# Up's block products with high and low operand halves in one matmul, and the norm factor applied in down

## The chip, the cores and the metric

The kernel runs on one core of a Trainium2 chip. The metric is the device time of one execution in microseconds; the median of several executions counts. The core has engines with queues of their own: TensorE (PE; its weight loads, PEld, overlap its matmuls), VectorE (DVE), ScalarE (ACT), GpSimd (POOL) and SyncE (SP, which issues most DMA transfers). They wait for each other through semaphores, and each takes its own queue in order.

## The reference, cut to what matters

One layer of a streaming encoder for 512 tokens and a model width of 2048. Token mixers and a cross-attention come first; the change concerns only the last step, the MLP:

```python
def _rmsnorm(x, gain, eps=NORM_EPS):
    y = xf * lax.rsqrt(jnp.mean(xf * xf, axis=-1, keepdims=True) + eps)
    return (y * gain.astype(jnp.float32)).astype(x.dtype)

hn = _rmsnorm(h, norm_mlp[l])
h = h + jnp.square(jax.nn.relu(hn @ mlp_w_up[l])) @ mlp_w_down[l]
out = _rmsnorm(h, norm_final)
```

`mlp_w_up` is 2048 x 8192 and `mlp_w_down` 8192 x 2048, all in 32-bit floats. The norm factor of a token, r = 1/sqrt(mean + eps), is a positive number, so relu(r u)^2 = r^2 relu(u)^2.

## The kernel before

**Precision.** A matmul here takes operands in a reduced 32-bit format (F32R). To keep the precision, each operand is split into a high half (a cast, on ScalarE) and a low half (operand minus high half, on VectorE): `split`, lines 128 to 136. A product then is three sums: high x high, high x low, low x high.

**Up.** `strassen` (line 1525) runs in 32 rounds, p = 0 to 31, of 256 output features each. It multiplies 2 x 2 blocks with seven block products in place of eight, named B11, B21, T1, T2, T3, B22, T4 by the operand on the activation's side (`comb`: seven combinations of eight tiles, made once; each tile holds the high half of 256 tokens in its columns HA and the low half in HB). The weights' side comes in each round: four 128 x 1024 blocks a11, a21, a22, a12 by DMA, and sums of them (s1, and in place) made by `add`, 1024 wide, on VectorE. `block` (line 1289) splits such an operand into tiles `whi` and `wlo`, two buffers each, and issues 24 matmuls of 256 columns: for each of 8 pieces of `whi`, one with HA and one with HB, then 8 pieces of `wlo` with HA. All 24 add up in the same 256 columns of a PSUM bank.

Three banks collect the products of a round: x takes B11, then T2, T3 and T4 on top, y takes T1 and then B22, z takes B21. After each product its sum so far is read: `S.copy` (ScalarE) or `add`/`sub` (VectorE) into the tiles c1 and c2 (128 x 512 each). A product that adds onto a bank waits until the reads of that bank are done. The products follow each other on TensorE as B11, T1, T2, B21, T3, B22, T4 (B21 is second in round 0). At the end of a round `done` (the function `square`, line 1652) makes c1 and c2 into relu(r c)^2: one VectorE operation (maximum or minimum with 0, times `rstd`, the factor r spread over all 128 rows, 512 tokens wide), and a Square on ScalarE. Four combinations of c1 and c2 follow on VectorE (tiles tt and t4), and DMA stores everything to a buffer in DRAM (`Cd`).

In round 0, `used` (line 1656) also computes r: a column sum by small matmuls (`pcol2`), Sqrt and reciprocal to the column tile `rcol`, and from it `rstd`: four diagonal tiles on VectorE, eight small matmuls into `prs` and a copy.

Beside this, rounds 2 to 17 transpose an old tile each on TensorE (`ht`, copied by ScalarE to `hr`), and up to round 30 a one-column copy to `ticks` lets GpSimd start background transfers.

**Down.** The stored tiles come back, are split, and `down` multiplies them with the down weights, again seven products, here with 512 output columns a matmul and tokens on the partitions. `into` (line 1698) adds finished banks to the residual tiles g, one VectorE addition of 128 x 512 each; the last product does the same in `last`. The final norm and the stores end the program.

**What sets the order.** A scheduler orders each engine's instructions when the program is built; the order below is the built program's.

Of the kernel before, what the change touches and what calls it, by code (L numbers as in the profile page):

```python
# [10 lines left out]
F32R = mybir.dt.float32r  # L11
# [6 lines left out]
P = 128  # L18
# [55 lines left out]
def build(tc, I, out):  # L74
# [1215 lines left out]
    def block(pt, a, parts, start):  # L1290
# [8 lines left out]
        for k in range(8):  # L1299
            PE.matmul(pt, lo[:, k * P:k * P + P], parts[k][0], start=False, stop=k == 7, skip_group_check=True)  # L1300

    def product(i, pt, a, start=True):
        block(pt[:, HA], a, [(comb[i][k][:, HA], comb[i][k][:, HB]) for k in range(8)], start)

# [220 lines left out]
    def strassen(p, done, used):  # L1525

        def product(i, pt, a, start=True):  # L1530
            block(pt[:, HA], a, [(comb[i][k][:, HA], comb[i][k][:, HB]) for k in range(8)], start)
            if used:
                used(i)

        if p == 0:
            a11, a12, a22, a21 = (raw(I["w_up"][p, i], o) for i, o in ((0, 1), (3, 1), (2, 1), (1, 0)))
        else:
            a11, a21, a22, a12 = (raw(I["w_up"][p, i]) for i in range(4))
        s1 = raw(None, 0 if p == 0 else None)
        x, y, z = (psb(f"up{n}{p}", t) for n, t in (("x", "mx"), ("y", "mg"), ("z", "mm")))  # L1540
        c1, c2 = sl2(), sl2()

# [12 lines left out]
        if p > 0:
            product(B21, z, a12)
            sub(c1[:, HA], c1[:, HA], z[:, HA])
        add(a12, a12, s1)
        product(T3, x, a21, False)
        add(c2[:, HB], c2[:, HB], x[:, HA])  # L1560
        product(B22, y, a12, False)
        add(c1[:, HB], c1[:, HB], y[:, HA])
        done(c1, ALU.min)
        product(T4, x, a22, False)
        S.copy(c2[:, HA], x[:, HA])  # L1565
        done(c2, ALU.max)
        t = pu.tile([P, T], F32, tag="tt", name=f"tt{p}", bufs=1)
        t4 = pu.tile([P, M], F32, tag="t4", name=f"t4_{p}", bufs=1)
        sub(t[:, HA], c1[:, HB], c1[:, HA])
        sub(c1[:, HB], c1[:, HB], c2[:, HB])  # L1570
        sub(t[:, HB], c1[:, HA], c1[:, HB])
        sub(t4, c2[:, HA], t[:, HB])
        if p > 1 and wanted:
            S.copy(ticks[:, p:p + 1], c2[:, 0:1])
            background(ticks[:, p:p + 1], 1)
        h = slice(p % 2 * M, p % 2 * M + M)
        v = lambda a: a.rearrange("p (a b) -> p a b", b=M)
        nc.scalar.dma_start(Cd[p // 2][:, 2:4, h], v(c2))
        nc.scalar.dma_start(Cd[p // 2][:, 0:2, h], v(c1))
        nc.sync.dma_start(Cd[p // 2][:, 4:6, h], v(t))  # L1580
        nc.sync.dma_start(Cd[p // 2][:, 6, h], t4)
# [65 lines left out]
        G[t][m] = ph.tile([P, 2, T], F32, tag=f"h{i // 2}{i % 2}", name=f"g{t}{m}", bufs=1)  # L1647
        nc.sync.dma_start(G[t][m], HTd[:, t, m * 1024:m * 1024 + 1024].rearrange("p (a b) -> p a b", b=T))

    diag = []  # L1650
    for p in range(32):
        def square(c, op):
            V.scalar_tensor_tensor(out=c, in0=c, scalar=0.0, in1=rstd, op0=op, op1=ALU.mult)
            S.activation(c, c, AF.Square)

        def used(i):
            if p == 0 and i == T3:
                pt = psb("pcol2", "scr", 1)
                for t in range(4):
                    op = PE.matmul(pt[:, t:t + 1], acc[:, t * P:(t + 1) * P], ones[:, 0:1], start=True, stop=True)  # L1660
                    if t == 0:
                        tc.keep_in_program_order(op)
                S.activation(rcol, pt[:, 0:4], AF.Sqrt, bias=b_eps6, scale=1.0 / 2048)
                V.reciprocal(out=rcol, in_=rcol)
                diag.append(sl2())
                for t in range(4):
                    V.tensor_scalar(out=diag[0][:, t * P:(t + 1) * P], in0=ident, scalar1=rcol[:, t:t + 1], scalar2=None, op0=ALU.mult)
            if p == 0 and i == B22:
                pt = psb("prs", "scg", 1)
                for t in range(4):  # L1670
                    op = PE.matmul(pt[:, t * P:(t + 1) * P], ones, diag[0][:, t * P:(t + 1) * P], start=True, stop=True)
                    if t == 0:
                        tc.keep_in_program_order(op)
                S.copy(rstd, pt)
            if p == 31 and i in (T1, T2, T3):
                for q in ((0,), (1, 2), (3,))[i - T1]:
                    piece_(0, 0, q)
# [20 lines left out]
    def into(half, blk, m, pts, op):  # L1698
        for t in (0, 1):
            g = G[2 * half + t][m][:, blk, :]  # L1700
            V.tensor_tensor(out=g, in0=g, in1=pts[t], op=op)

    def down(c, i, q, pts, a, start):
        cnt[0] += 1
# [41 lines left out]
    def last(c):  # L1746
        kept = {}
        done = [(t, n) for n in range(4) for t in (2, 3)]
        for t in (0, 1):
            for m, q in both:  # L1750
# [15 lines left out]
                        gained(1, n)  # L1766
                if q == 3:
                    g = G[t][m][:, 1, :]
                    V.tensor_tensor(out=g, in0=g, in1=X[m][t], op=ADD)
                    square_of(t, 1, m)  # L1770
                    if t == 1 and m == 0:
                        gained(1, 1)
# [185 lines left out]
```

## Time and profile before

| | |
|---|---|
| median of 3 runs | 2951.33 us (2949.74 to 2951.42) |
| profiled execution, its own time | 2950.02 us |
| its span | 2948.3 us |
| PE busy | 2914.1 us (99%) |
| PEld busy | 2538.3 us (86%) |
| DVE busy | 2163.4 us (73%) |
| ACT busy | 1530.7 us (52%) |
| POOL busy | 312.6 us (11%) |

The span is the profiled execution from first to last instruction; its own time is 1.7 us longer. Busy shares are means over stages: the projections and mixers take the first 1.3 ms, up runs from 1663 to 2324 us, down from there to the end. In the timelines, a row is start and length in us, engine, line, operation, out<-in, shape and count, and in brackets the idle time before it with what ended it.

### The profile page before, as it was taken

Reading aid. Unit: us, or ns where it says so; the run is one execution under the profiler, and the core shown is the slowest. Engines: PE = TensorE matmul, PEld = TensorE weight load, DVE = VectorE, ACT = ScalarE, POOL = GpSimd, SP = SyncE. Lnnn points to the kernel's source line nnn. Section 1 sums busy time; section 2 is a strip of 40 time slices with the busy share of each in tenths; the row PEclk is TensorE's granted clock in tenths of the full one; section 3 lists DMA queues with packets and bytes.
Section 4 is the critical chain, followed back from the end, with each engine's and each line's share of the span. In section 5 each row is a group of like instructions: output and inputs, shape, how many; then the busy total and the mean of one; then the engine's idle time right before and its main releaser. Section 6 shows DMA issues by size and latency. Waiting matters only on the chain.

```text
span 2948.3 us, 52595 instructions
## 1 busy us (share of the span) xinstructions
PE 2914.1 (99%) x20866; PEld 2538.3 (86%) x20866; DVE 2163.4 (73%) x3114; ACT 1530.7 (52%) x2160; POOL 312.6 (11%) x704
## 2 busy tenths in 40 slices
PE   9999999999999999999999999999999999999998
PEld 7887787787778898879988899999999878888887
DVE  7676676676677746767856788888888897878776
ACT  6554545555556555664445545454444555454544
POOL 0302203213113000001111000000100000000000
PEclk9999999999999999999999999999999999999999
DMA  5332433323425588787788667778777878686755
GB/s 180 107 92 79 105 87 84 98 88 85 125 79 154 160 257 303 243 268 203 197 224 194 177 192 214 216 221 249 210 196 204 270 263 268 215 264 220 253 187 189
DMA packets 304520, 546.93 MB, mean 186 GB/s; under 512 B 97224, under 2 KB 178380, under 8 KB 303248
## 3 DMA queue, kind: packets, MB, share of 16 engines
q1 hardware_dynamic: 245264, 449.17, 48.3%
q0 software_dynamic: 35840, 67.12, 11.2%
q10 hardware_dynamic: 23168, 27.27, 2.6%
q8 instruction: 164, 2.69, 0.4%
q14 instruction: 84, 0.69, 0.1%
HBM read 479.10 MB, written 131.48 MB: 207 GB/s over the span
## 4 chain that ended last, share of the span: by engine, by line
PE 61%; DMA 3%; DVE 3%; ACT 1%; issue 1%; SPq 0%; DVEq 0%; ACTq 0%
PE upx L1297 8%; PE upy L1297 4%; PE upx L1300 4%; PE dx L1711 3%; PE dx L1712 3%; PE dx L1714 3%; PE kq L249 3%; PE kp L249 3%; PE vp L122 3%; PE sc L122 3%; PE at L122 3%; PE vo L122 2%; PE opx L1297 2%; PE upy L1300 2%; PE upz L1297 2%; PE dy L1714 2%
## 5 line engine op out<-in xcount | busy, mean ns | idle before, releaser
L130 ACT CAST whi<-ub 128x1024 fp32r<-128x1024 f32 x291 | 305.5, 1051 | 358.3 <-PE upx L1297 87.3
L131 DVE TENSOR_TENSOR wlo<-ub,whi 128x1024 fp32r<-128x1024 f32 x291 | 355.1, 1222 | 76.4 <-ACT whi L130 72.3
L249 PE MATMUL py<-xhi,whi 128*128 128x512 f32 x928 | 370.8, 400 | 7.0 <-ACT xhi L249 7.0
L249 PE MATMUL py<-xhi,wlo 128*128 128x512 f32 x928 | 377.3, 407 | 0.0
L249 PE MATMUL py<-xlo,whi 128*128 128x512 f32 x928 | 371.8, 401 | 0.0
L130 ACT CAST whi<-ua 128x1024 fp32r<-128x1024 f32 x205 | 215.5, 1051 | 262.6 <-PE upx L1297 72.6
L249 ACT CAST whi<-wraw 128x1024 fp32r<-128x1024 f32 (+1 forms) x180 | 188.0, 1045 | 234.1 <-PE py L249 183.0
L249 DVE TENSOR_TENSOR wlo<-wraw,whi 128x1024 fp32r<-128x1024 f32 (+1 forms) x180 | 224.4, 1247 | 96.3 <-ACT whi L249 93.9
L131 DVE TENSOR_TENSOR wlo<-ua,whi 128x1024 fp32r<-128x1024 f32 x205 | 250.4, 1222 | 58.5 <-ACT whi L130 57.1
L1297 PE MATMUL upx<-cb,whi 128*128 128x256 f32 x2048 | 269.4, 285 | 1.5 <-ACT whi L130 1.5
L1297 PEld LDWEIGHTS upx<-cb,whi 128*128 128x128 f32 x2048 | 256.1, 193 | 1.8 <-ACT whi L130 1.7
L249 PEld LDWEIGHTS py<-xhi,whi 128*128 128x128 f32 x928 | 175.4, 189 | 41.0 <-ACT xhi L249 7.0
L249 PEld LDWEIGHTS py<-xlo,whi 128*128 128x128 f32 x928 | 175.1, 189 | 37.9 <-issue 1.0
L249 PEld LDWEIGHTS py<-xhi,wlo 128*128 128x128 f32 x928 | 175.5, 189 | 33.2 <-issue 1.0
L1711 PE MATMUL dx<-whi,dh 128*128 128x512 f32 x480 | 187.2, 390 | 1.3 <-ACT sl L1565 0.8
L1712 PE MATMUL dx<-whi,dl 128*128 128x512 f32 x480 | 186.8, 389 | 0.0
L1300 PE MATMUL upx<-cb,wlo 128*128 128x256 f32 x1024 | 143.8, 283 | 0.3 <-DVE wlo L131 0.3
L1297 PE MATMUL upy<-cb,whi 128*128 128x256 f32 x1024 | 133.7, 283 | 1.8 <-ACT whi L130 1.8
L131 DVE TENSOR_TENSOR wlo<-wraw,whi 128x1024 fp32r<-128x1024 f32 x80 | 97.9, 1224 | 48.6 <-ACT whi L130 47.2
L1300 PEld LDWEIGHTS upx<-cb,wlo 128*128 128x128 f32 x1024 | 132.1, 192 | 0.5 <-DVE wlo L131 0.5
L1297 PEld LDWEIGHTS upy<-cb,whi 128*128 128x128 f32 x1024 | 127.5, 192 | 2.2 <-ACT whi L130 2.2
L1714 PE MATMUL dx<-wlo,dh 128*128 128x512 f32 x480 | 128.6, 389 | 0.0
(865 smaller groups left out, 6681.6 us busy)
## 6 DMA issues: line engine op xcount, KB each, us to landing
ws<-in_w_dn POOLq DMA_DIRECT2D x128, 512.0 KB, 7.2
wraw<-in_w_in SPq DMA_DIRECT2D x116, 512.0 KB, 3.6
ua<-in_w_dn SPq DMA_DIRECT2D x108, 512.0 KB, 4.2
ub<-in_w_up SPq DMA_DIRECT2D x72, 512.0 KB, 4.8
ua<-in_w_up SPq DMA_DIRECT2D x56, 512.0 KB, 4.6
ub<-in_w_dn SPq DMA_DIRECT2D x52, 512.0 KB, 4.4
sl<-cd SPq DMA_DIRECT2D x104, 256.0 KB, 4.4
ub<-ws SPq DMA_DIRECT2D x52, 512.0 KB, 4.4
```

The lines of the kernel that those rows point to most:

```text
L122: PE.matmul(o, l, r, start=start, stop=stop)
L130: tie(S.copy(hi, src))
L131: V.tensor_tensor(out=lo, in0=src, in1=hi.bitcast(F32), op=ALU.subtract)
L249: f(*a, **k)
L1297: PE.matmul(pt, hi[:, k * P:k * P + P], x, start=start, stop=False, skip_group_check=True)
L1300: PE.matmul(pt, lo[:, k * P:k * P + P], parts[k][0], start=False, stop=k == 7, skip_group_check=True)
L1711: PE.matmul(pts[t], uh[:, x], hi[:, w], start=start and z == 0 and q == 0, stop=False, skip_group_check=True)
L1712: PE.matmul(pts[t], ul[:, x], hi[:, w], start=False, stop=False, skip_group_check=True)
L1714: PE.matmul(pts[t], uh[:, x], lo[:, w], start=False, stop=z == 1 and q == 3, skip_group_check=True)
```

## The change

Three things change in up and one in down.

1. `product` in `strassen` calls the new function `wide` instead of `block`. For each of 8 pieces of `whi` it issues one matmul with the whole `comb` tile, 512 columns, so that high x high lands in the bank's first half and high x low in its second; the 8 matmuls with `wlo` stay 256 columns wide. A product has 16 matmuls. The two halves of a bank must now be summed: each of the seven reads gets one more VectorE operation, 256 wide, that adds or subtracts the second half.
2. `square` no longer multiplies by `rstd`: it is Relu (with scale -1 for c1, 1 for c2) and Square, both on ScalarE. The 512-wide VectorE operation is gone.
3. In round 0, `rstd` is not made (no diagonal tiles, no `prs` matmuls, no copy); `rcol` is squared, and `nrcol` is its negative.
4. In down, `into` and `last` multiply the bank by a column of `rcol` or `nrcol` while they add it: a three-operand VectorE operation in place of the addition.

```diff
+    def wide(pt, a, parts, start):
...
+        split(a, hi, lo)
+        for k in range(8):
+            PE.matmul(pt, hi[:, k * P:k * P + P], parts[k], start=start and k == 0, stop=False, skip_group_check=True)
+        for k in range(8):
+            PE.matmul(pt[:, HA], lo[:, k * P:k * P + P], parts[k][:, HA], start=False, stop=k == 7, skip_group_check=True)
...
         def product(i, pt, a, start=True):
-            block(pt[:, HA], a, [(comb[i][k][:, HA], comb[i][k][:, HB]) for k in range(8)], start)
+            wide(pt, a, comb[i], start)
...
         product(B11, x, a11)
         S.copy(c1[:, HA], x[:, HA])
+        add(c1[:, HA], c1[:, HA], x[:, HB])
...
         product(T1, y, s1)
         S.copy(c2[:, HB], y[:, HA])
+        add(c2[:, HB], c2[:, HB], y[:, HB])
...
         product(T2, x, s1, False)
         S.copy(c1[:, HB], x[:, HA])
+        add(c1[:, HB], c1[:, HB], x[:, HB])
...
             product(B21, z, a12)
             sub(c1[:, HA], c1[:, HA], z[:, HA])
+            sub(c1[:, HA], c1[:, HA], z[:, HB])
...
         product(T3, x, a21, False)
         add(c2[:, HB], c2[:, HB], x[:, HA])
+        add(c2[:, HB], c2[:, HB], x[:, HB])
         product(B22, y, a12, False)
         add(c1[:, HB], c1[:, HB], y[:, HA])
-        done(c1, ALU.min)
+        add(c1[:, HB], c1[:, HB], y[:, HB])
+        done(c1, -1.0)
         product(T4, x, a22, False)
         S.copy(c2[:, HA], x[:, HA])
-        done(c2, ALU.max)
+        add(c2[:, HA], c2[:, HA], x[:, HB])
+        done(c2, 1.0)
...
-        def square(c, op):
-            V.scalar_tensor_tensor(out=c, in0=c, scalar=0.0, in1=rstd, op0=op, op1=ALU.mult)
+        def square(c, sign):
+            S.activation(c, c, AF.Relu, scale=sign)
             S.activation(c, c, AF.Square)
...
                 V.reciprocal(out=rcol, in_=rcol)
-                diag.append(sl2())
-                for t in range(4):
-                    V.tensor_scalar(out=diag[0][:, t * P:(t + 1) * P], in0=ident, scalar1=rcol[:, t:t + 1], scalar2=None, op0=ALU.mult)
-            if p == 0 and i == B22:
-                pt = psb("prs", "scg", 1)
...
-                S.copy(rstd, pt)
+                V.tensor_tensor(out=rcol, in0=rcol, in1=rcol, op=ALU.mult)
+                V.tensor_scalar(out=nrcol, in0=rcol, scalar1=-1.0, scalar2=None, op0=ALU.mult)
...
     def into(half, blk, m, pts, op):
         for t in (0, 1):
             g = G[2 * half + t][m][:, blk, :]
-            V.tensor_tensor(out=g, in0=g, in1=pts[t], op=op)
+            i = 2 * half + t
+            f = (nrcol if op is SUB else rcol)[:, i:i + 1]
+            V.scalar_tensor_tensor(out=g, in0=pts[t], scalar=f, in1=g, op0=ALU.mult, op1=ALU.add)
...
-                    V.tensor_tensor(out=g, in0=g, in1=X[m][t], op=ADD)
+                    V.scalar_tensor_tensor(out=g, in0=X[m][t], scalar=rcol[:, t:t + 1], in1=g, op0=ALU.mult, op1=ALU.add)
```

The scheduler's order at three places follows, before and after. On TensorE, product T4 of round 4: the last two pieces of its high half and the first four of its low half. Before:

```order
L1297 MATMUL upx4_18734<-cb4_6_17020,whi830_18919 128x256 x2
L1297 MATMUL upx4_18734<-cb4_7_17713,whi830_18919 128x256 x2
L1300 MATMUL upx4_18734<-cb4_0_17014,wlo830_18920 128x256
L1300 MATMUL upx4_18734<-cb4_1_17015,wlo830_18920 128x256
L1300 MATMUL upx4_18734<-cb4_2_17016,wlo830_18920 128x256
L1300 MATMUL upx4_18734<-cb4_3_17017,wlo830_18920 128x256
```

After:

```order
L1308 MATMUL upx4_18529<-cb4_6_17020,whi829_18672 128x512
L1308 MATMUL upx4_18529<-cb4_7_17713,whi829_18672 128x512
L1310 MATMUL upx4_18529<-cb4_0_17014,wlo829_18673 128x256
L1310 MATMUL upx4_18529<-cb4_1_17015,wlo829_18673 128x256
L1310 MATMUL upx4_18529<-cb4_2_17016,wlo829_18673 128x256
L1310 MATMUL upx4_18529<-cb4_3_17017,wlo829_18673 128x256
```

The pair of 256-column matmuls on one piece (x2) has become one of 512; the low half and the sequence of products are as they were.

On ScalarE, the end of round 4: the rows run from the cast for T1 of round 5 (`whi834`) to that for T2 (`whi835`); sl822 and sl823 are c1 and c2 of round 4, L1654 is Square, L1565 and L1544 read bank x. Before:

```order
L130 CAST whi834_19016<-ub70_18980 128x1024
L1654 ACTIVATE sl822_18737<-sl822_18737 128x512
L1565 COPY sl823_18738<-upx4_18734 128x256
L1642 COPY hr0_2_18969<-ht0_2_18964 128x512
L1654 ACTIVATE sl823_18738<-sl823_18738 128x512
L1574 COPY ticks_14226<-sl823_18738 128x1
L1578 DMA cd2_187<-sl823_18738 128x2x256
L1544 COPY sl831_18984<-upx5_18981 128x256
L130 CAST whi835_19046<-ub70_18980 128x1024
```

After, between the same two casts (now `whi833` and `whi834`), with c1 and c2 as sl821 and sl822; L1670 is Relu, L1671 Square:

```order
L130 CAST whi833_18755<-ub70_18726 128x1024
L1670 ACTIVATE sl821_18532<-sl821_18532 128x512
L1582 COPY sl822_18533<-upx4_18529 128x256
L1671 ACTIVATE sl821_18532<-sl821_18532 128x512
L1660 COPY hr0_2_18715<-ht0_2_18710 128x512
L1670 ACTIVATE sl822_18533<-sl822_18533 128x512
L1671 ACTIVATE sl822_18533<-sl822_18533 128x512
L1592 COPY ticks_14226<-sl822_18533 128x1
L1596 DMA cd2_187<-sl822_18533 128x2x256
L1597 DMA cd2_187<-sl821_18532 128x2x256
L1554 COPY sl830_18730<-upx5_18727 128x256
L130 CAST whi834_18778<-ub70_18726 128x1024
```

Two Relu operations have come in, and both stores of c1 and c2 now stand ahead of the cast for T2 (`whi834`), where one stood before. In rounds 3, 5, 10, 12 and 17 the Relu of c1 stands ahead of the cast for the next T1 as well.

On VectorE at the same place, from the read of B22 in bank y to the low half for T2 of round 5 (`wlo833`, 834 and 835 belong to B11, T1 and T2 of round 5). Before:

```order
L1263 TENSOR_TENSOR sl822_18737<-sl822_18737,upy4_18735 128x256
L131 TENSOR_TENSOR wlo833_18987<-ub66_18972,whi833_18986 128x1024
L1653 SCALAR_TENSOR_TENSOR sl822_18737<-sl822_18737,rstd_201 128x512
L131 TENSOR_TENSOR wlo834_19017<-ub70_18980,whi834_19016 128x1024
L1653 SCALAR_TENSOR_TENSOR sl823_18738<-sl823_18738,rstd_201 128x512
L1260 TENSOR_TENSOR tt4_18950<-sl822_18737 128x256
L1263 TENSOR_TENSOR ub70_18980<-ub70_18980,ub66_18972 128x1024
L1260 TENSOR_TENSOR sl822_18737<-sl822_18737,sl823_18738 128x256
L1260 TENSOR_TENSOR tt4_18950<-sl822_18737 128x256
L1260 TENSOR_TENSOR t4_4_18951<-sl823_18738,tt4_18950 128x256
L131 TENSOR_TENSOR wlo835_19047<-ub70_18980,whi835_19046 128x1024
```

After, with c1 and c2 as sl821 and sl822 and the three low halves as `wlo832`, 833 and 834:

```order
L1263 TENSOR_TENSOR sl821_18532<-sl821_18532,upy4_18530 128x256
L131 TENSOR_TENSOR wlo832_18733<-ub66_18718,whi832_18732 128x1024
L1263 TENSOR_TENSOR sl821_18532<-sl821_18532,upy4_18530 128x256
L131 TENSOR_TENSOR wlo833_18756<-ub70_18726,whi833_18755 128x1024
L1263 TENSOR_TENSOR sl822_18533<-sl822_18533,upx4_18529 128x256
L1260 TENSOR_TENSOR tt4_18696<-sl821_18532 128x256
L1263 TENSOR_TENSOR ub70_18726<-ub70_18726,ub66_18718 128x1024
L1260 TENSOR_TENSOR sl821_18532<-sl821_18532,sl822_18533 128x256
L1260 TENSOR_TENSOR tt4_18696<-sl821_18532 128x256
L1260 TENSOR_TENSOR t4_4_18697<-sl822_18533,tt4_18696 128x256
L1263 TENSOR_TENSOR sl830_18730<-sl830_18730,upx5_18727 128x256
L131 TENSOR_TENSOR wlo834_18779<-ub70_18726,whi834_18778 128x1024
```

The scalings by rstd are gone; the second read of y stands between the low halves of B11 and T1, the read of T4's second half (`sl822`<-`upx4`) behind the low half of T1, and the read of round 5's B11 (`sl830`<-`upx5`) ahead of the low half of T2.

More of the change, by code (lines that the diff above doesn't have):

```diff
@@ L1300, in block @@
             PE.matmul(pt, lo[:, k * P:k * P + P], parts[k][0], start=False, stop=k == 7, skip_group_check=True)
+    def wide(pt, a, parts, start):
+        cnt[0] += 1
+        hi = pw.tile([P, 1024], F32R, tag="whi", name=f"whi{cnt[0]}", bufs=NWS)
+        lo = pw.tile([P, 1024], F32R, tag="wlo", name=f"wlo{cnt[0]}", bufs=NWS)
+        split(a, hi, lo)
[3 more added lines that the diff above has]
+            PE.matmul(pt[:, HA], lo[:, k * P:k * P + P], parts[k][:, HA], start=False, stop=k == 7, skip_group_check=True)
     def product(i, pt, a, start=True):
@@ L1557, in strassen @@
             sub(c1[:, HA], c1[:, HA], z[:, HA])
+            sub(c1[:, HA], c1[:, HA], z[:, HB])
         add(a12, a12, s1)
@@ L1648, in held @@
         nc.sync.dma_start(G[t][m], HTd[:, t, m * 1024:m * 1024 + 1024].rearrange("p (a b) -> p a b", b=T))
-    diag = []
     for p in range(32):
-        def square(c, op):
-            V.scalar_tensor_tensor(out=c, in0=c, scalar=0.0, in1=rstd, op0=op, op1=ALU.mult)
+        def square(c, sign):
+            S.activation(c, c, AF.Relu, scale=sign)
             S.activation(c, c, AF.Square)
@@ L1664, in used @@
                 V.reciprocal(out=rcol, in_=rcol)
-                diag.append(sl2())
-                for t in range(4):
-                    V.tensor_scalar(out=diag[0][:, t * P:(t + 1) * P], in0=ident, scalar1=rcol[:, t:t + 1], scalar2=None, op0=ALU.mult)
-            if p == 0 and i == B22:
-                pt = psb("prs", "scg", 1)
[L1670 to L1673, printed above, removed]
-                S.copy(rstd, pt)
+                V.tensor_tensor(out=rcol, in0=rcol, in1=rcol, op=ALU.mult)
+                V.tensor_scalar(out=nrcol, in0=rcol, scalar1=-1.0, scalar2=None, op0=ALU.mult)
             if p == 31 and i in (T1, T2, T3):
```

## The prediction

> **What bounds the kernel now.** I read the stages first. The three rows are busy time by stage: the MLP's up stage from its second of 32 rounds on (two rows), then down. The columns are window, length, PE, PEld, DVE, ACT and POOL busy with their instructions, granted clock, DMA share, GB/s.
>
> ```profile
> 1690.00:2050.00 360.00, 359.71 (x3004) 359.51 (x3003) 296.55 (x353) 180.24 (x262) 30.18 (x47) 1.00 0.75 214
> 2050.00:2326.00 276.00, 275.28 (x2289) 274.66 (x2287) 230.45 (x276) 137.69 (x195) 24.23 (x37) 1.00 0.76 212
> 2326.00:2948.00 622.00, 610.86 (x2683) 502.75 (x2683) 485.34 (x541) 302.92 (x375) 0.00 (x0) 1.00 0.72 237
> ```
>
> In up TensorE is idle for 360.00 - 359.71 + 276.00 - 275.28 = 1.0 us of 636, at full clock. VectorE is busy 82 to 84% and ScalarE 50%. So a shorter stream on TensorE shortens this stage, as long as VectorE, which the change loads further, keeps up. That is the whole question, so I read TensorE's timeline through the end of round p = 4 (start, length, line, tiles, count). `ht` is the transpose of one old tile, which stands only in rounds 2 to 17.
>
> ```profile
> 1770.04 2.08 PE L1297 MATMUL upx<-cb,whi 128*128 128x256 f32 x16
> 1771.96 1.12 PE L1300 MATMUL upx<-cb,wlo 128*128 128x256 f32 x8
> 1772.92 0.60 PE L1638 MATMUL ht<-cst,h 128*128 128x128 f32 x4
> 1773.28 2.16 PE L1297 MATMUL upx<-cb,whi 128*128 128x256 f32 x16
> ...
> 1776.24 2.08 PE L1297 MATMUL upy<-cb,whi 128*128 128x256 f32 x16
> ...
> 1779.12 2.08 PE L1297 MATMUL upx<-cb,whi 128*128 128x256 f32 x16
> ```
>
> Starts count here, since the lengths overlap. One product (T1, 1776.24 to 1779.12) takes 2.88 us for 24 matmuls of 256 columns: **120.0 ns each**, 16 on the high half in 1.92 us and 8 on the low half in 0.96. `ht` adds 1776.24 - 2.88 - 1772.92 = 0.44 us. The same kernel has 512-column matmuls with a weight load each, just ahead of up; these are the first and last of a run of 36:
>
> ```profile
> 1654.70 0.39 PE L122 MATMUL at<-phi,whi 128*128 128x512 f32 x1
> ...
> 1662.63 0.39 PE L122 MATMUL at<-phi,wlo 128*128 128x512 f32 x1
> ```
>
> 35 steps in 7.93 us: **226.6 ns each**, 13.4 ns less than two of 256.
>
> **TensorE's part.** A product becomes 8 x 226.6 + 8 x 120.0 = 2773 ns, 1813 on the high half and 960 on the low: 107 ns less. 31 rounds of 7 products give 217 x 0.107 = **23.2 us**, if TensorE stays the bound.
>
> Round 0 is held by other things (below, its waits), so I count half its 0.75 us, 0.4. It also loses the eight small matmuls that spread the norm factor:
>
> ```profile
> 1670.40 2.18 PE L1297 MATMUL upy<-cb,whi 128*128 128x256 f32 x16 [1.64 <-ACT whi L130]
> 1673.61 1.21 PE L1300 MATMUL upy<-cb,wlo 128*128 128x256 f32 x8 [1.02 <-DVE wlo L131]
> ...
> 1687.66 1.05 PE L1671 MATMUL prs<-sl,cst 128*128 128x128 f32 x8
> 1688.46 2.15 PE L1297 MATMUL upx<-cb,whi 128*128 128x256 f32 x16
> ```
>
> 1688.46 - 1687.66 = **0.8 us** on TensorE's own stream. Round 0's first waits stem from weights that land late and from the last operand splits; the extra additions there may cost 1 us or free as much, and I put them at 0 with 2 us either side.
>
> **VectorE's part.** Durations come from the same place, the end of round 4:
>
> ```profile
> 1770.24 0.42 DVE L1263 TENSOR_TENSOR sl<-sl,upy 128x256 f32<-128x256 f32 x1 [0.21 <-PE upy L1300]
> ...
> 1773.24 1.22 DVE L131 TENSOR_TENSOR wlo<-ub,whi 128x1024 fp32r<-128x1024 f32 x1 [0.84 <-ACT whi L130]
> 1774.39 0.68 DVE L1653 SCALAR_TENSOR_TENSOR sl<-sl,rstd 128x512 f32<-128x512 f32 x1
> 1774.99 0.42 DVE L1260 TENSOR_TENSOR tt<-sl 128x256 f32<-128x256 f32 x1
> 1775.32 1.22 DVE L1263 TENSOR_TENSOR ub<-ub,ub 128x1024 f32<-128x1024 f32 x1
> 1776.46 0.42 DVE L1260 TENSOR_TENSOR sl<-sl,sl 128x256 f32<-128x256 f32 x1
> 1776.91 0.42 DVE L1260 TENSOR_TENSOR tt<-sl 128x256 f32<-128x256 f32 x1
> ```
>
> From start to start, a 1024-wide operation takes 1.15 us, a 512-wide one 0.60, a 256-wide one 0.33, and 0.46 where the next needs its result. A round has 11 wide ones (7 low halves, 4 sums), 3 reads of PSUM, 4 combinations and 2 scalings with rstd. The change adds 7 reads of PSUM and drops the scalings: 7 x 0.33 - 2 x 0.60 = **+1.1 us**. The new total is 11 x 1.15 + 14 x 0.33 + 2 x 0.13 = 17.5 us in a round of 7 x 2.773 = 19.4 (19.85 with `ht`): 90%. It fits with 1.9 us to spare, but waits in VectorE's fixed order must fit there too, so I walked the tightest place.
>
> **The tightest place** is the end of a round. Let H be the end of T4's high half (1771.96 above). ScalarE there:
>
> ```profile
> 1772.16 1.05 ACT L130 CAST whi<-ub 128x1024 fp32r<-128x1024 f32 x1 [1.83 <-PE upx L1297]
> 1773.12 0.63 ACT L1654 ACTIVATE sl<-sl 128x512 f32<-128x512 f32 x1
> 1773.65 0.35 ACT L1565 COPY sl<-upx 128x256 f32<-128x256 f32 x1
> 1773.90 0.59 ACT L1642 COPY hr<-ht 128x512 f32<-128x512 f32 x1
> 1775.10 0.63 ACT L1654 ACTIVATE sl<-sl 128x512 f32<-128x512 f32 x1 [0.62 <-DVE sl L1653]
> 1775.77 0.19 ACT L1574 COPY ticks<-sl 128x1 f32<-128x1 f32 x1
> 1775.77 0.37 ACTq L1578 DMA_DIRECT2D cd<-sl  x1
> ```
>
> Steps read off: TensorE's end to a reader, 0.20; cast to next 0.96, cast to its low half on VectorE 1.08; 512-wide function to next 0.53, to one that needs it 0.67; copy to next 0.25; DMA issue 0.37. In the changed order: cast for next T1 at H+0.20, Relu c1 1.16, copy c2 1.69, Square c1 1.94, `hr` 2.47. VectorE takes that T1's low half at H+1.28 and then the new addition to c2 at 2.43; that ends at 2.85, so Relu c2 starts at 3.00, Square c2 3.67, ticks 4.34, two DMA issues to 5.09, copy of the next c1 5.10, cast for the next T2 5.35, ready at 6.43. TensorE, undisturbed, comes to that T2 at H + 0.96 + 0.44 + 2 x 2.773 = 6.95. **It is in time by 0.5 us**, and the other new condition there, next c1's addition before T2 may write onto x, ends at about 5.9, 1.0 us early. Where T4 writes onto x after T3, the two additions to c2 with T4's low half between end 0.20 + 0.33 + 1.15 + 0.42 = 2.10 us after T3, and B22 gives 2.77: 0.7 us early. So the added waits cost nothing while VectorE is not behind; without that cover each 0.1 us of lateness costs 31 x 0.1 = 3.1 us.
>
> Five rounds (3, 5, 10, 12, 17) have Relu c1 ahead of the cast on ScalarE. It needs c1's last addition, at about H+0.45, so the cast is late by 0.8 and T2 by 0.2: 5 x 0.2 = **1.0 us lost**. Late weights are covered no worse: the one such wait in the steady rounds was a sum behind a load of 8.18 us,
>
> ```profile
> 1879.54 8.18 DMA ub<-in_w_up
> ```
>
> that cost TensorE 0.29 us,
>
> ```profile
> 1890.21 1.21 PE L1300 MATMUL upx<-cb,wlo 128*128 128x256 f32 x8 [0.29 <-DVE wlo L131]
> ```
>
> and this sum now stands later in VectorE's queue.
>
> **Where up meets down.** Down's first block writes onto the bank that T4 of the last round held:
>
> ```profile
> 2325.66 0.35 ACT L1565 COPY sl<-upx 128x256 f32<-128x256 f32 x1
> 2326.06 0.50 PE L1711 MATMUL dx<-whi,dh 128*128 128x512 f32 x1 [0.78 <-ACT sl L1565]
> ```
>
> TensorE waited 0.78 us for the copy; now it also waits for an addition on a VectorE that splits down's operands besides. Bounds: 0 (the addition ready by then) and two wide operations ahead of it, 2.3; I take **1.0 us**.
>
> **Down.** Its 108 additions turn into the three-operand form with a column factor:
>
> ```profile
> L1701 DVE TENSOR_TENSOR g<-g,dx 128x512 f32<-128x512 f32 x60 | 38.5, 683 | 17.9 <-PE dx L1714 17.9
> L1739 DVE SCALAR_TENSOR_TENSOR g<-g,rt,gain 128x512 f32<-128x512 f32 x12 | 8.2, 749 | 0.1
> ```
>
> 112 x (749 - 683) = 7.4 us on VectorE, which is idle for 137 us of this stage; only the last, with the final norm behind it, is on the path: 0.1 us.
>
> **The sum**, against the profiled execution (span 2948.3, its own time 2950.0): 23.2 + 0.4 + 0.8 - 1.0 - 1.0 - 0.1 = 22.3 us less, 2927.7. The median shown, 2951.3, is 1.3 above that execution, so I say **2929 us**. With round 0 at either end, the seam at 0 or 2.3 and the five rounds free or doubled, the forecast's own range is 2924 to 2934.
>
> **Rivals.**
> - *Part of it eaten by the ScalarE chain.* My walk has 0.5 us to spare; if issues or the extra functions take 0.8 us more than read off, each T2 waits 0.3: 31 x 0.3 = 9.3 us back, 2938. For it: eleven steps in a row, two kinds of them (Relu, a second issue) not in that order before. Against: each step has a row. 12%.
> - *VectorE becomes the bound.* If the operations don't overlap as the starts show, a round takes 11 x 1.22 + 14 x 0.42 = 19.3 us, and with the 0.84 us wait for the cast that stays, 20.1: as long as now, 2950. Against: 1774.99 to 1775.32 is 0.33 for an operation that lasts 0.42. 6%. [...]
> - *A 512-column matmul is no cheaper here than two of 256*, so the change doesn't do on TensorE what it says: 2950. The 36 rows above speak against it. 3%. The Trainium skill, "TensorE: Matmul & The Clock Gate", section "Back-to-back issue gap", has a warm gap of N/2.4 + 2.5 ns, so a pair would save 2.5 ns and the whole about 4.5 us, an estimate from that page; the trace has 13.4.
> - *Slower: a convoy at the end of each round.* The addition to c2 is new between T4 and Relu c2, and next T2's cast stands behind Relu, Square and the issues. If VectorE reaches it two wide operations late (2.3 us) in every round, T2 waits 2.3 - 0.5 = 1.8 and the round loses 1.05 net of its 0.75: 31 x 1.05 = 33 us, 2984. It decides against the change from 1.25 us late on. For it: 90% load in a fixed order. Against: 1.9 us of slack a round to catch up. 6%.
>
> **How the numbers follow.** Forecast 73%, the others as given. 0.2%, 5.9 us, is about what a measurement of this kernel can tell from no change. Faster by more: forecast and first rival, 85%; within: second and third, 9%; slower: the last, 6%. The range must hold 8 in 10: the forecast with 2 us more below, for a better round 0, and the first rival with some room: 2922 to 2943.
>
> **What would show it.** Right: the step between products 2.77 us; from round 1 on TensorE idle for little more than 1 us; VectorE at about 90% of up; down's seam wait near 1.8 us; the small matmuls gone. Wrong: TensorE waits at T2's first matmul for the cast (first rival) or at x for an addition (last), or VectorE without idle time in up (second), or a high half still at 1.92 us (third).

## The result, and the profile after

| | median | runs | fastest to slowest |
|---|---|---|---|
| before, same chips | 2950.53 us | 6 | 2947.09 to 2955.29 |
| after | 2935.57 us | 6 | 2934.69 to 2941.63 |

The ratio after/before is 0.9947, with a 95% interval of 0.9937 to 0.9958. The change saves 15 us. 2929 had been predicted, within 2922 to 2943: direction and range hold, but a third of the expected 22.3 us did not come. The time lies outside 2924 to 2934, the forecast's own range; the stated range holds it only through the room that it left for the first rival, which expected 2938. The profiled execution of after took 2936.28 us, its span is 2934.5.

The stages of the changed kernel, with the columns of the table that the prediction opens with; the first row is the same stretch as there, the second ends at 2310, shortly before up does (2314):

```profile
1690.00:2050.00 360.00, 357.21 (x2059) 313.45 (x2059) 318.24 (x452) 200.20 (x300) 27.51 (x48) 1.00 0.74 218
2050.00:2310.00 260.00, 258.68 (x1476) 226.73 (x1475) 234.04 (x333) 144.26 (x213) 20.72 (x37) 1.00 0.74 212
```

TensorE still bounds up, but is now idle for 4.1 us of 620, where it was 1.0 of 636; and 0.7 of that 1.0 was the wait where up meets down, so in up itself it was 0.3. VectorE is busy 88 and 90%, as forecast. So two questions stand: what a product takes, and where the idle time is. TensorE's timeline, changed kernel, T1, T2 and what follows:

```profile
1850.25 2.00 PE L1308 MATMUL upy<-cb,whi 128*128 128x512 f32 x8
1852.09 1.11 PE L1310 MATMUL upy<-cb,wlo 128*128 128x256 f32 x8
1853.05 2.00 PE L1308 MATMUL upx<-cb,whi 128*128 128x512 f32 x8
1854.89 1.12 PE L1310 MATMUL upx<-cb,wlo 128*128 128x256 f32 x8
1855.84 0.60 PE L1656 MATMUL ht<-cst,h 128*128 128x128 f32 x4
```

From start to start the high half takes 1.84 us, not 1.813, and the low half 0.95 to 0.96; over a round of seven products without `ht` (19.55 us) a product is **2.793 us, not 2.773**. The single starts in the trace, as means over the steps without a wait, show where: the eight wide matmuls (512 columns) take 233, 235, 229, 233, 231, 227, 227 and 227 ns, the eight narrow ones (256 columns) 114, 119 and then 120. The wide ones are slow behind the narrow ones of the product before.

The tightest place, ScalarE at the end of round 4 of the changed kernel. H, the end of T4's high half, is 1774.45 here:

```profile
1774.65 1.05 ACT L130 CAST whi<-ub 128x1024 fp32r<-128x1024 f32 x1 [1.74 <-DVE wlo L131]
1775.60 0.62 ACT L1670 ACTIVATE sl<-sl 128x512 f32<-128x512 f32 x1
1776.13 0.35 ACT L1582 COPY sl<-upx 128x256 f32<-128x256 f32 x1
1776.38 0.63 ACT L1671 ACTIVATE sl<-sl 128x512 f32<-128x512 f32 x1
1776.92 0.57 ACT L1660 COPY hr<-ht 128x512 f32<-128x512 f32 x1
1777.38 0.64 ACT L1670 ACTIVATE sl<-sl 128x512 f32<-128x512 f32 x1
1778.05 0.63 ACT L1671 ACTIVATE sl<-sl 128x512 f32<-128x512 f32 x1
1778.72 0.19 ACT L1592 COPY ticks<-sl 128x1 f32<-128x1 f32 x1
1778.72 0.40 ACTq L1596 DMA_DIRECT2D cd<-sl  x1
1779.21 0.44 ACTq L1597 DMA_DIRECT2D cd<-sl  x1
1779.69 0.37 ACT L1554 COPY sl<-upx 128x256 f32<-128x256 f32 x1 [0.79 <-DVE tt L1260]
1779.96 1.05 ACT L130 CAST whi<-ub 128x1024 fp32r<-128x1024 f32 x1
```

The walk forecast these starts after H: 0.20, 1.16, 1.69, 1.94, 2.47, 3.00, 3.67, 4.34, the issues to 5.09, 5.10, 5.35. Measured: 0.20, 1.15, 1.68, 1.93, 2.47, 2.93, 3.60, 4.27, the issues to 5.20, 5.24, 5.51. The cast for T2 is done at H + 6.56 and TensorE comes at H + 6.98: 0.42 us to spare, 0.5 forecast.

Down begins without a wait on the banks; up's last matmuls and down's first, changed kernel:

```profile
2313.33 1.11 PE L1310 MATMUL upx<-cb,wlo 128*128 128x256 f32 x8
2314.28 0.40 PE L1722 MATMUL dx<-whi,dh 128*128 128x512 f32 x1
2314.51 0.40 PE L1723 MATMUL dx<-whi,dl 128*128 128x512 f32 x1
```

Five stretches of the two profiled executions add up to the difference of the spans. B21 of round 1 (bank z) marks where the disturbed beginning of up ends; below, a round is counted from one B21 to the next:

| stretch | before | after | difference |
|---|---|---|---|
| ahead of up | 1662.9 | 1668.4 | +5.5 |
| up, to B21 of round 1 | 37.2 | 35.3 | -1.9 |
| up, from there to down (214 products) | 623.9 | 610.5 | -13.4 |
| down, first to last matmul | 616.0 | 611.4 | -4.6 |
| after the last matmul | 8.3 | 8.8 | +0.5 |
| span | 2948.3 | 2934.5 | -13.8 |

The first line is a surprise, since the order of instructions ahead of up is the same in both programs.

### The profile page after: what moved, and what is told of

Its sections match the earlier page's. It is cut to its first block, busy times and chain, and to the rows that moved or that the text cites. A ratio compares the mean times of both kernels' runs of the same rounds, so it can differ in the third digit from the quotient of the medians.

```text
span 2934.5 us, 49236 instructions
## 1 busy us (share of the span) xinstructions
PE 2896.1 (99%) x19066; PEld 2442.6 (83%) x19066; DVE 2195.8 (75%) x3272; ACT 1561.4 (53%) x2223; POOL 305.3 (10%) x704
## 4 chain that ended last, share of the span: by engine, by line
PE 60%; DMA 3%; DVE 3%; ACT 2%; issue 1%; SPq 0%; ACTq 0%; DVEq 0%
PE upx L1308 8%; PE upx L1310 4%; PE upy L1308 4%; PE dx L1725 3%; PE dx L1723 3%; PE dx L1722 3%; PE kp L249 3%; PE sc L122 3%; PE at L122 3%; PE vp L122 3%; PE kq L249 3%; PE vo L122 2%; PE opx L1297 2%; PE upz L1308 2%; PE dy L1722 2%; PE upy L1310 2%
## 5 line engine op out<-in xcount | busy, mean ns | idle before, releaser
L1308 PE MATMUL upx<-cb,whi 128*128 128x512 f32 x1024 | 259.0, 395 | 4.7 <-ACT whi L130 4.5
L1308 PEld LDWEIGHTS upx<-cb,whi 128*128 128x128 f32 x1024 | 184.0, 189 | 40.4 <-ACT whi L130 6.9
L1310 PEld LDWEIGHTS upx<-cb,wlo 128*128 128x128 f32 x1024 | 139.4, 190 | 10.2 <-DVE wlo L131 0.3
L1308 PE MATMUL upy<-cb,whi 128*128 128x512 f32 x512 | 128.5, 393 | 2.8 <-ACT whi L130 2.8
L249 ACT ACT_TABLE_LOAD x86 | 110.3, 1283 | 26.4 <-DVE suml_gn L249 11.9
```

The source lines that it names most:

```text
L249: f(*a, **k)
L1308: PE.matmul(pt, hi[:, k * P:k * P + P], parts[k], start=start and k == 0, stop=False, skip_group_check=True)
L1310: PE.matmul(pt[:, HA], lo[:, k * P:k * P + P], parts[k][:, HA], start=False, stop=k == 7, skip_group_check=True)
```

## The experiments

All medians stand beside runs of the kernel before on the same chip. "Steady up" is the third line of the table above.

**1 and 2: each part alone.** First the wide products alone; the diff against the changed kernel:

```
-            S.activation(c, c, AF.Relu, scale=sign)
+            V.scalar_tensor_tensor(out=c, in0=c, scalar=0.0, in1=rstd, op0=op, op1=ALU.mult)
...
-            V.scalar_tensor_tensor(out=g, in0=pts[t], scalar=f, in1=g, op0=ALU.mult, op1=ALU.add)
+            V.tensor_tensor(out=g, in0=g, in1=pts[t], op=op)
```

> Only the wide products of the change; the scalings with rstd in up and the plain additions in down are as before. Measure: up from its first matmul to down's first (before 661.1 us, changed kernel 645.9 us, each in one profile), and a round without ht (20.16 and 19.55). VectorE then has 17.5 + 2 x 0.60 = 18.7 us of work in a round of 19.55, 96%. Theory A, TensorE's own stream sets the round: rounds stay at 19.55, only the eight prs matmuls come back (0.8), up about 647, total about 2937. Theory B, VectorE is close to being the bound and the dropped scalings were what made room: rounds of 20 us and more, up 655 or more, total 2945 or more.

2942.68 us against 2949.30, ratio 0.9977 (0.9967 to 0.9987). Steady up 612.0 us, 11.9 less than before, most rounds at 19.55 and 20.00. (Three matmuls of B21 of round 1 come early here, and the count starts behind them; from the first of them it is 613.6, 10.3 less.) Its two windows of up:

```profile
1690.00:2050.00 360.00, 356.58 (x2061) 313.32 (x2060) 338.84 (x488) 182.23 (x265) 28.94 (x47) 1.00 0.75 217
2050.00:2316.00 266.00, 263.18 (x1500) 230.56 (x1500) 253.90 (x365) 132.75 (x190) 25.66 (x37) 1.00 0.75 212
```

VectorE is busy 94 and 95%, and the rounds still come at TensorE's pace, except for single waits for a cast (5.5 us in nine). Theory A, with more of these waits than it had; VectorE is not the bound at 95%. The total is 5.7 us above what A gave; 4.1 of it is a longer down (see below).

Then the norm factor's part alone:

```
-            wide(pt, a, comb[i], start)
+            block(pt[:, HA], a, [(comb[i][k][:, HA], comb[i][k][:, HB]) for k in range(8)], start)
...
-        add(c1[:, HA], c1[:, HA], x[:, HB])
```

> Only the norm factor's part of the change: Relu and Square on ScalarE, the factor in down's additions; products in 24 matmuls of 256 columns as before. Theory A, TensorE's stream sets up: rounds stay at 20.16 without ht, up loses the prs matmuls only, 661.1 - 0.8 = 660.3 us, and the seam's 0.9; total about 2949. Theory B, the short round 0 of the changed kernel (27.6 us to round 1's second product, 31.4 before) comes from VectorE and ScalarE having less to do ahead of it, not from the products: round 0 is 2 to 3 us shorter here too, up 657 to 658, total about 2947.

2946.51 against 2949.30, ratio 0.9992 (0.9982 to 1.0003): no difference that these runs can tell. Steady up 623.3; its first stretch 37.9, no shorter than before. Theory A. So the products carry the saving in up; the other part makes room, which up hardly needs.

**3: no narrow matmuls.**

```
-            PE.matmul(pt[:, HA], lo[:, k * P:k * P + P], parts[k][:, HA], start=False, stop=k == 7, skip_group_check=True)
+            PE.matmul(pt, lo[:, k * P:k * P + P], parts[k], start=False, stop=k == 7, skip_group_check=True)
```

> The low half of each operand also runs over all 512 columns, which adds the product of the two low halves; so a product is 16 matmuls of 512 columns and no run of 256-column ones stands between. In the changed kernel the first five wide matmuls behind such a run take 233, 235, 229, 233 and 230 ns, the last three 227. Theory A, it is the passage from narrow to wide that costs: all 16 take 227 ns, a product 3.63 us, and rounds of 25.4 without a stall. Theory B, wide matmuls are slower wherever VectorE and ScalarE write beside them: 230 ns or more at most places, a product 3.68 us or more. Time by A: 217 x (3.626 - 2.795) = 180 us longer, about 3115.

3116.23 us in one run. Its timeline, columns as above:

```profile
1819.77 1.98 PE L1310 MATMUL upy<-cb,wlo 128*128 128x512 f32 x8
1821.59 1.98 PE L1308 MATMUL upx<-cb,whi 128*128 128x512 f32 x8
1823.40 1.98 PE L1310 MATMUL upx<-cb,wlo 128*128 128x512 f32 x8
1825.21 0.60 PE L1656 MATMUL ht<-cst,h 128*128 128x128 f32 x4
```

Eight wide matmuls take 1.81 to 1.82 us, high or low half; the single starts are 227 ns at all 16 places, and rounds are 25.39 without a stall. VectorE and ScalarE execute as many operations a round as in the changed kernel, though spread over a longer round; and in the changed kernel itself the last three wide matmuls of a product take 227 ns beside the same writes. So theory B falls: the forecast's 226.6 ns was right for a stream of wide matmuls, and it is narrow ones ahead of them that cost.

**4: the order held.**

```
-            PE.matmul(pt, hi[:, k * P:k * P + P], parts[k], start=start and k == 0, stop=False, skip_group_check=True)
+            op = PE.matmul(pt, hi[:, k * P:k * P + P], parts[k], start=start and k == 0, stop=False, skip_group_check=True)
+            if k == 0:
+                tc.keep_in_program_order(op)
```

> The first matmul of each product is held to the order in which the program is written, so that no two matmuls of the next round's first product come to stand ahead of T4 in five rounds (3, 5, 10, 12, 17), and Relu c1 stands behind the cast there. Theory A: the 0.45 us by which these five rounds are longer comes from those two matmuls, which wait for their cast; the rounds are 20.00 like the others with ht, up 645.9 - 2.2 = 643.6. Theory B, the 0.45 comes from Relu c1 and the additions being late, whatever TensorE's order: the rounds stay at 20.4, up at 645.9. The total differs too little to tell: 2933 or 2935.5.

2932.09 against 2949.30, ratio 0.9945 (0.993 to 0.996). Round 3 of the changed kernel, from B22 on:

```profile
1749.37 2.00 PE L1308 MATMUL upy<-cb,whi 128*128 128x512 f32 x8
1751.21 1.11 PE L1310 MATMUL upy<-cb,wlo 128*128 128x256 f32 x8
1752.51 2.56 PE L1308 MATMUL upx<-cb,whi 128*128 128x512 f32 x10 [0.19 <-ACT whi L130]
1754.91 1.12 PE L1310 MATMUL upx<-cb,wlo 128*128 128x256 f32 x8
1755.87 0.60 PE L1656 MATMUL ht<-cst,h 128*128 128x128 f32 x4
```

and of this one (its line numbers are two higher behind the first matmul):

```profile
1749.18 2.00 PE L1308 MATMUL upy<-cb,whi 128*128 128x512 f32 x8
1751.02 1.11 PE L1312 MATMUL upy<-cb,wlo 128*128 128x256 f32 x8
1751.97 2.00 PE L1308 MATMUL upx<-cb,whi 128*128 128x512 f32 x8
1753.81 1.12 PE L1312 MATMUL upx<-cb,wlo 128*128 128x256 f32 x8
1754.77 0.60 PE L1658 MATMUL ht<-cst,h 128*128 128x128 f32 x4
```

The `x10` gives it away: two matmuls of the next round's B11 stand ahead of T4's eight and wait for a cast that has just begun. 1752.51 - 1751.21 = 1.30 us in place of 0.95. Without them four of the five rounds are 20.00, round 12 is 20.09, and steady up is 608.1, 2.4 less than in the changed kernel. Theory A. Holding the order also moved Relu c1 behind the cast on ScalarE, so two things changed; but in the changed kernel that cast came at H + 0.25 in all five rounds, only 0.05 later than in round 4, where Relu stands behind it, and the wait shown is TensorE's only one in the round. Up as a whole (644.9) missed the forecast 643.6, because its first stretch took 36.8 us this time.

**5 and 6: narrow matmuls put between the wide ones**, to win the loss back; both with the order held. The loop of experiment 5 (experiment 6 lets the low half start four matmuls later: `8 + 4`, `k >= 4` and `j = k - 4`):

```
+        for k in range(8 + 0):
+            if k < 8:
+                op = PE.matmul(pt, hi[:, k * P:k * P + P], parts[k], start=start and k == 0, stop=False, skip_group_check=True)
...
+            if k >= 0:
+                j = k - 0
+                PE.matmul(pt[:, HA], lo[:, j * P:j * P + P], parts[j][:, HA], start=False, stop=j == 7, skip_group_check=True)
```

> In each product the wide matmuls on the high half and the narrow ones on the low half alternate, one and one; the first matmul of each product is held to its place as in in_order. The low half is needed 1.6 us earlier and the high half is given back 0.9 us later, so waits for operands are expected and only the steps between matmuls that follow without a wait count. Theory A: weight loads come 120 ns apart at the closest, a run of eight narrow matmuls uses up their lead, and the next wide ones pay; with a pair every 340 ns the lead is never used up: wide 227, narrow 113, a product without waits 2.72. Theory B: every wide matmul that follows a narrow one takes 233 to 236: a product 8 x (234 + 113) = 2.78 or more.

> As in_order, with three of a product's eight narrow matmuls moved in between its last four wide ones (five wide, narrow, wide, narrow, wide, narrow, wide, five narrow). Theory A (a run of narrow matmuls uses up the lead of the weight loads, single ones don't): 8 x 227 + 3 x 113 + 113 + 119 + 3 x 120 = 2747 ns and a rest of the passage, 2.75 to 2.77 for a product in place of 2.795. Theory B (each passage from narrow to wide costs 7 ns): 2.81. The high half is given back 0.3 us later, and the cast for T2 has less than 0.1 us to spare in the rounds without ht, so there the wait for it takes back about what the product gains: those rounds 19.5 to 19.6 by A, those with ht 19.7 to 19.8 in place of 20.0. Up 639 to 642 by A (in_order 644.9), 647 or more by B.

2998.64 us in one run, and 2949.69 against 2952.33 (ratio 0.9989, 0.9981 to 0.9998). Inside a product of the first, without a wait:

```profile
2106.18 0.40 PE L1309 MATMUL upz<-cb,whi 128*128 128x512 f32 x1
2106.42 0.28 PE L1314 MATMUL upz<-cb,wlo 128*128 128x256 f32 x1
2106.54 0.40 PE L1309 MATMUL upz<-cb,whi 128*128 128x512 f32 x1
```

A pair takes 0.35 to 0.36 us, a product of eight pairs 2.8: theory B. In the second, with its shorter mixing, the three wide matmuls that follow a single narrow one take 232 to 241 ns, and a product 2.80 us. So my picture of weight loads that use up a lead falls: the first wide matmul behind a narrow one is slow, after one as after eight. Waits for operands did the rest, since the low half is needed earlier and the high half given back later; in experiment 6 they bring up to 659.8 us, far above the 639 to 642 of theory A; theory B had said 647 or more.

**7 and 8: two stores moved from ScalarE's queue to SP's**, against the late casts for T2 in rounds 23 and 30; both with the order held, 8 together with experiment 6.

```
-        nc.scalar.dma_start(Cd[p // 2][:, 2:4, h], v(c2))
-        nc.scalar.dma_start(Cd[p // 2][:, 0:2, h], v(c1))
+        nc.sync.dma_start(Cd[p // 2][:, 2:4, h], v(c2))
+        nc.sync.dma_start(Cd[p // 2][:, 0:2, h], v(c1))
```

> As in_order, with the stores of c1 and c2 issued on SP's queue, so that the two issues (0.37 to 0.43 us each, and their wait for the combinations) no longer stand on ScalarE ahead of the cast for T2. Theory A, the prediction's tightest place: rounds 23 and 30 of the changed kernel lose 0.49 us each because this cast is late behind a store's issue; the rounds are 19.55 now, up about 1 us less than in_order's 644.9. Theory B, they are late because VectorE comes late with the sums: the two rounds stay at 20.04.

> woven4 and stores_sp together: the product of 2.75 to 2.77 us with about 0.8 us more room on ScalarE ahead of T2's cast. Theory A: no round waits for that cast; rounds of 7 x 2.76 = 19.3 us without ht and 19.8 with it, up 644.9 - 31 x 0.25 - 1 = 636, total about 2924 (in_order 2932). Theory B, VectorE is the bound by then (17.5 us of 19.3, 91%, and the low half needed 0.9 us earlier): waits for the low half, rounds of 19.55 or more, total 2931 or more.

2960.47 us in one run, and 2960.83 against 2952.33 (ratio 1.0035, 1.0024 to 1.0047): slower than the kernel before. TensorE's waits in up, experiment 7 (total us, times, longest):

```profile
PE upx L1308 <- DVE sl L1263: 17.7, 14, 2.1
PE upx L1308 <- ACT whi L130: 0.5, 2, 0.3
```

The wait for the cast is nearly gone and another has come. It stands ahead of T4 in 13 of the 14 cases (17.4 of the 17.7 us): T4 writes onto x, and so waits until VectorE has read T3 there. One of them, on SP, VectorE and TensorE (rows from three timelines):

```profile
2069.68 0.38 SPq L1598 DMA_DIRECT2D cd<-sl  x1
2071.79 0.44 SPq L1287 DMA_DIRECT2D ub<-in_w_up  x1
2079.76 1.23 DVE L1263 TENSOR_TENSOR ub<-ua,ub 128x1024 f32<-128x1024 f32 x1 [3.05 <-issue]
2085.30 0.42 DVE L1263 TENSOR_TENSOR sl<-sl,upx 128x256 f32<-128x256 f32 x1
2085.87 2.85 PE L1308 MATMUL upx<-cb,whi 128*128 128x512 f32 x8 [2.14 <-DVE sl L1263]
```

From 2063.2 on SP waits at the first moved store for its tile, until 2069.68. The next load of weights stands behind the stores on that queue and is issued at 2071.79; in experiment 4 the same load goes out ahead of the stores that SP issues. It lands at 2079.68, 0.08 us before VectorE's sum begins. VectorE was idle for 3.05 us until then, and the read of T3 that T4 waits for is late with everything behind that sum. In all 13 cases the load has changed places with the stores in this way, the sum begins 0.08 to 0.12 us after its landing, and T4's wait ends 6.1 us after the sum's start. In experiment 8 the waits for an addition stand ahead of T4 too. Neither theory had this. Steady up is 635.8 us, 27.7 more than with the order held alone.

For the casts that it was made for, the run does tell something: rounds 2, 23 and 30, at 20.03 and 20.04 in the changed kernel and with the order held, are 19.55 here, as theory A had it. The prediction's slower rival had a late addition ahead of T2; what came is a late addition ahead of T4, through a late load.

**9 to 12: what is chance?** Both kernels once more, unchanged, the changed kernel with plain additions in down, and experiment 4 again. The diff of the plain additions is the second half of experiment 1's, here with the norm factor left out.

> The kernel before, unchanged, for a second profile of it. In the first one up begins at 1662.9 us, in the profiles of the changed kernel and its variants at 1665.4 to 1668.5, though the program ahead of up is the same; and down, first to last matmul, takes 616.0 us against 610.3 to 612.4 in all that have both parts of the change. Theory A: the start of up differs from one execution to the next (here anywhere between 1662 and 1669), while down's 616 belongs to the kernel (615 to 617 again). Theory B: both are chance, and down may come out at 612; or both belong to the kernel, and up begins at 1662.9 within 0.5.

> The changed kernel, unchanged, for a second profile and more times. Theory A: what the first profile showed belongs to it: products of 2.795 us, five rounds of 20.45, rounds 23 and 30 of 20.04, up 644.5 to 647 (round 0 moves by 1.5 us from one execution to the next), down 610 to 612.5, total 2935.5. Theory B: the five rounds or the 4.6 us less in down were chance of that execution: 20.00 in the rounds, or 615 and more in down.

> The changed kernel with plain additions in down, as before the change: the norm factor is left out of the result. 112 operations on VectorE take 683 ns in place of about 700 to 750. Theory A, the prediction: these operations are hidden, blocks of 10.88 us in down and 610 to 612.5 us from its first to its last matmul, up as in the changed kernel (644.5 to 647), total within 1 us of it. Theory B: the three-operand form itself is what made down's start 4.6 us shorter: down at 615 to 616, total 2939 to 2940.

> in_order, unchanged, beside after_again on the same chip. By its first profile up is 1.0 us shorter than in the changed kernel, where the five rounds alone give 5 x 0.45 = 2.2 and round 0 took 1.5 us more. Theory A: 2.2 us less in the median than after_again, within what the chip varies: a difference of 1 to 4 us, about 2932 to 2934 against 2935.5. Theory B: no difference, 0 to 1 us.

| kernel | median | ratio, 95% | ahead of up | up's first stretch | steady up | down |
|---|---|---|---|---|---|---|
| before, first and second profile | 2951.33, 2945.43 | | 1662.9, 1662.2 | 37.2, 34.5 | 623.9, 623.7 | 616.0, 615.0 |
| after, first and second | 2935.57, 2936.61 | 0.9943 (0.993 to 0.9957), second | 1668.4, 1667.5 | 35.3, 40.1 | 610.5, 610.1 | 611.4, 610.6 |
| plain additions in down | 2937.05 | 0.9948 (0.9934 to 0.9962) | 1668.1 | 35.3 | 611.1 | 612.1 |
| order held, first and second | 2932.09, 2931.75 | 0.9936 (0.9924 to 0.9949), second | 1666.8, 1669.8 | 36.8, 35.4 | 608.1, 608.1 | 610.3, 610.9 |
| wide products alone | 2942.68 | 0.9977 (0.9967 to 0.9987) | 1668.4 | 36.5 | 612.0 | 615.5 |
| norm factor's part alone | 2946.51 | 0.9992 (0.9982 to 1.0003) | 1665.4 | 37.9 | 623.3 | 615.5 |

Steady up repeats within 0.5 us, with the five long rounds and the three late casts (rounds 2, 23 and 30) at the same places each time. Its first stretch doesn't: 35.3 and 40.1 in one and the same kernel, which put up as a whole, 650.2 in the second profile, outside theory A's 644.5 to 647. Of the kernel before neither theory held as written: up began at 1662.2 again and down took 615.0, so both seem to belong to it. In down the three-operand form costs nothing that shows, nor does it bring the shorter start (theory A): the additions with bank dx are 683 ns in the plain form,

```profile
L1710 DVE TENSOR_TENSOR g<-g,dx 128x512 f32<-128x512 f32 x60 | 38.5, 683 | 16.7 <-PE dx L1723 16.7
```

and 744 and 746 in the changed kernel,

```profile
L1712 DVE SCALAR_TENSOR_TENSOR g<-dx,nrcol,g 128x512 f32<-128x512 f32 x32 | 22.5, 744 | 9.7 <-PE dx L1725 9.7
L1712 DVE SCALAR_TENSOR_TENSOR g<-dx,rcol,g 128x512 f32<-128x512 f32 x28 | 19.7, 746 | 8.0 <-PE dx L1725 8.0
```

while down's later blocks take 10.88 us in both, apart from a few in either. Experiment 4 repeated gives 2931.75 (2931.41 to 2934.92) beside 2936.61 (2929.82 to 2940.68) for the changed kernel on that chip. The runs overlap, and the medians differ by 4.9, more than either theory had; that it is the better version by some 2 us rests on steady up, 608.1 twice against 610.5 and 610.1.

## Why the prediction was right, and where its sum was off

**TensorE's stream is the bound: right.** The change shortens it, the gain comes from the products (experiment 1 against 2), and up stays at TensorE's pace. A high half takes 1.84 us, not 1.92, so the third rival is out.

**"107 ns less" a product: mis-sized; it is 87.** The step added a time read in a run of wide matmuls only to one read in a run of narrow ones only, 8 x 226.6 + 8 x 120.0. Both were right for their runs (experiment 3 has the first again at 227), but the product passes from one to the other, and the first five wide matmuls behind the narrow ones cost 27 ns more, of which the first narrow ones give back some 6. 214 products x 0.020 = 4.3 us of steady up's shortfall.

**TensorE "idle for little more than 1 us": wrong, 4.1.** Steady up saved 13.4 where the steps give 214 x 0.107 - 1.0 = 21.9. Products account for 4.3 of the missing 8.5; the other 4.2 are waits:
- *The five rounds.* The step had them lose 0.2 each because Relu stands ahead of a cast and makes it late by 0.8; measured, the cast is late by 0.05. They lose 0.45, and through something else: two matmuls of the next B11 ahead of T4 (experiment 4). I had looked for the changed order on ScalarE, where Relu stands, and not on TensorE. 5 x 0.25 = 1.25 more than forecast.
- *Rounds 2, 23 and 30*, 0.48 or 0.49 each. The walk through the tightest place was right to 0.2 us in each step, but I made it in a round with `ht`, which gives TensorE's next product 0.44 us of delay. Most rounds without it keep up. In these three ScalarE has the copy of the next B11 ahead of Square c2 and waits 0.29 us for TensorE there, so the stores and the cast for T2 behind them are late (round 23, ScalarE and then TensorE), in every profile of the changed kernel:

```profile
2138.38 0.37 ACT L1554 COPY sl<-upx 128x256 f32<-128x256 f32 x1 [0.29 <-PE upx L1310]
2138.65 0.63 ACT L1671 ACTIVATE sl<-sl 128x512 f32<-128x512 f32 x1
2140.25 1.05 ACT L130 CAST whi<-ua 128x1024 fp32r<-128x1024 f32 x1 [0.74 <-DVE tt L1260]
2140.02 1.11 PE L1310 MATMUL upy<-cb,wlo 128*128 128x256 f32 x8
2141.35 2.11 PE L1308 MATMUL upx<-cb,whi 128*128 128x512 f32 x8 [0.22 <-ACT whi L130]
```

With the stores taken off ScalarE's queue these rounds are 19.55 (experiment 7). That is the first rival's chain, in three rounds of 31.
- *Round 31 with the end of 30*, about 1.9 us, which no step had: ScalarE's casts stand there behind operands for down that come from memory, as in the longest case:

```profile
2306.63 0.63 ACT L133 ACTIVATE dh<-cr 128x512 fp32r<-128x512 f32 x1 [3.16 <-DMA cr<-cd]
2308.25 2.10 PE L1308 MATMUL upy<-cb,whi 128*128 128x512 f32 x8 [0.79 <-ACT whi L130]
```

These come to 4.6 us. In its first profile the kernel before had lost 0.65 in waits itself, so about 4.0 of the 4.2 are named.

**Round 0 (0.4) and the prs matmuls (0.8): not to be told.** Up's first stretch varies by 5 us between executions of one kernel. The 2 us either side that I gave it were too few.

**VectorE: right.** 90% forecast, 88 and 90% measured, and at 95% TensorE was still the bound (experiment 1). The second and the last rival did not come in the changed kernel.

**The seam, "1.0 us" lost: wrong.** TensorE waited 0.78 us in the first profile of the kernel before, not at all in its second, and in neither of the changed kernel's. So the seam took nothing, and gave back 0.9 us at most. Before, five matmuls wrote to the first of down's banks ahead of the first onto T4's bank; in the changed program nine do. The new addition is hidden behind those four. I took the place of the wait for given, though the change had moved it.

**Down's 0.1: right for the additions, but down is 4.6 us shorter** (4.4 by the second profiles, where neither kernel waits at the seam). In the first profiles all of it, the seam's 0.9 included, is in its first 180 us. The same stretch of 116 us from down's first matmul on, before:

```profile
2323.90:2440.00 116.10, 112.40 (x489) 90.84 (x489) 101.70 (x119) 63.23 (x82) 0.00 (x0) 1.00 0.84 279
```

and after:

```profile
2314.20:2430.00 115.80, 115.10 (x504) 93.40 (x503) 104.45 (x122) 65.84 (x86) 0.00 (x0) 1.00 0.86 292
```

TensorE is idle 3.7 and 0.7 us there, at 279 and 292 GB/s. Every profile with the wide products and without the scalings with rstd has down at 612.4 or less, plain additions or not; either part alone has 615.5, the kernel before 616.0 and 615.0. So it belongs to the change, but by which step was not isolated.

**Ahead of up, 5.5 us more, is open.** The two profiles of the kernel before begin up at 1662.9 and 1662.2, the twelve others between 1665.4 and 1669.8; ahead of up the order of instructions is the same before and after. Two against twelve is hardly chance, yet nothing that I ran tells the cause. It took back about what down gave.

So the sum, 22.3 forecast and 13.8 between the two profiled spans, missed by 8.5. Steady up alone missed by as much. Down with the seam came out 5.7 better than forecast (4.6 gained where the terms lost 1.1), and the stretch ahead of up 5.5 worse, with no term at all. That these two cancel, and that the total stayed within the stated range, is luck.

## What to carry to other kernels

Time an instruction in the mixture in which it will run: two rates read from pure runs, added, overstated this gain by almost a quarter. A kernel whose order a scheduler makes has to be compared on every engine where the prediction has a wait; the two matmuls ahead of T4 and the four at the seam were both in the changed program, and both bore on a term. And a tight wait is walked in its tightest variant (here a round without `ht`, with the copy ahead of Square).

## What had not been expected of the hardware

- The first wide matmul (512 columns) behind a narrow one (256) takes 232 to 241 ns in place of 227, whether one narrow one stood ahead of it or eight (experiment 6); after eight it takes five wide ones until 227 is reached. Of eight narrow ones behind wide ones the first takes 114 ns, the second 119, the others 120 (changed kernel). Why is open; that the loads of weights use up their lead was tried and fell (experiment 5).
- The Trainium skill, "TensorE: Matmul & The Clock Gate", section "Back-to-back issue gap", gives 131 ns a matmul at 512 columns in a stream of loads and matmuls, and N/2.4 + 2.5 ns for a single one. No run here, with F32R operands, agrees with either: 227 ns in pure runs with a load each (experiment 3), 11 more than the second figure's 216.
- VectorE is busy 94 and 95% over 626 us without becoming the bound (experiment 1). Experiment 7 has it at 86 and 84% (310.73 of 360.00 and 243.68 of 289.00 us), and there TensorE waits for it, because sums ahead of the awaited additions wait for a late load: what VectorE waits for decided, not how busy it is.
